# Hybrid encoder with experts on one core: one operand of convolutions, series and norms in PSUM, idle products on TensorE, GpSimd's splits behind the norm's root

## Chip, cores and metric

The kernel runs on one core of a Trainium2 chip. The metric is the time of one execution on the device in microseconds; a lower number is better. The engines are called PE (TensorE), DVE (VectorE), ACT (ScalarE), POOL (GpSimd) and SP (SyncE, which issues most DMAs).

## What is computed

The reference is a stack of two layers on 256 tokens of width 1024, all in float32. A layer mixes tokens in three branches, merges them with gates, and applies 32 SwiGLU experts, of which each token uses two.

```python
h = _layernorm(x, ln0_g, ln0_b)
for l in range(DEPTH):                       # DEPTH = 2
    mix = _mixer(h, w_in[l], ...)            # projections, three branches, gates, w_out
    h = _layernorm(DN_ALPHA * h + mix, ln1_g[l], ln1_b[l])
    ffn = _moe(h, w_router, router_bias, w1[l], w3[l], w2[l])
    h = _layernorm(DN_ALPHA * h + ffn, ln2_g[l], ln2_b[l])
...
# branch A: grouped-query attention; q and k get an RMS norm per head and an axial rotary turn
q = _axial_rope(_rms(q, q_g), tables) * (HEAD_DIM ** -0.5)
k = _axial_rope(_rms(k, k_g), tables)
# branch C: gated delta rule; q, k, v first pass a short convolution and SiLU
qkv = jax.nn.silu(_short_conv(jnp.concatenate([q, k, v], axis=-1), conv_w))   # 5 taps
g = -jnp.exp(A_log) * jax.nn.softplus(aa + dt_bias)                           # decay
# experts
hid = jax.nn.silu(xt @ w1[e]) * (xt @ w3[e])
y = y + comb[:, e:e + 1] * (hid @ w2[e])
```

The mixer's projections go in the order ga0, cqk, cz, cv, akv, aq, ga1, bqk, ...: cqk and cv are q, k and v of branch C, akv and aq the keys, values and queries of branch A, ga a gate.

## The kernel before

**Layers and tiles.** Tokens lie on the partitions in two tiles of 128 (t = 0, 1). Each layer has a mixer (about 265 us) and an expert stage (about 440 us). Weights are streamed from HBM by SP into rings; the slots of the experts' slabs come free as earlier work is done with what lies there.

**Splits.** Matrix products are made from a high and a low part. `split` (L186) casts a block of weights to the high part (ACT, `uh_...`) and subtracts it from the block for the low part (`ul_...`), on DVE or POOL. Products with three such terms follow on PE. A projection's weights come in four blocks u, two k steps each. `cut()` makes the next split of the stream, `take()` hands out the block.

**Order.** PE's order is written out by the program (`pinned`). The order on DVE, ACT and POOL is made by a scheduler; each engine works through its own queue in order.

**The mixer's first part.** `norm(t)` normalises tile t: `bn` takes statistics, `rsqrt` (L229) makes the root on POOL, `centred` (L252) subtracts the mean and multiplies by the gain, `shifted` (L257) multiplies by the root and adds the bias. Then `turn_in` transposes the tile (tp; the high part placeT, the low part placeU) and ga0 runs on it. `conv(i, b)` (L537) works on a bank b of 128 x 512 (two channel groups of 256 tokens): ACT copies it from PSUM into `placeH` (L541), DVE makes five taps for each group (one `ts`, four `stt`, into placeA or placeB), ACT takes tanh, DVE multiplies (into placeB or placeC).

`delta_line` (L608) makes the decay g. The logarithm in softplus is a series of eleven DVE operations on 128 x 16 elements, in the buffer shown as `gap`. From g follow POOL's products placeG and placeC and PE's products eb and db. `norm_rope` (L555) is the RMS norm and rotary turn of a key or query; for the key it runs twice (t = 0, 1) and ends in placeG. `key_line` then transposes the keys (kTA) on PE. The names placeA to placeU are ring places that several tensors share in turn.

**The expert stage.** After the mixer's norm, the router's choice `both` is made on DVE, the products `rk` count ranks, `select` makes the permutation P, `gather` brings tokens to the experts (xg on PE, copied to h), and `weigh` makes the weighted W, whose transpose is PT. Then for every expert: `up` (PE products named h), `down` (PE products named mo into two column halves n = 0, 1, evicted as the high part op by ACT and the low part by DVE), and for every second `combine` (my). After the last expert come the statistics of `my` and the next layer's norm, or the final one.

```python
for hf in range(2):                                   # down(e)
    w2 = slab()
    for j in range(2):
        for n in range(2):
            mm(bs[n][n * 64:n * 64 + 64], hidT[e][:, j, hf * 64:hf * 64 + 64],
               w2[:, j, n * 512:(n + 1) * 512], hf == 0 and j == 0, hf == 1 and j == 1)
```

In layer 1 three splits of ga0's blocks are issued ahead of the first norm, which is ordered behind the first of them (on DVE); the two others are POOL's ul_ga.

## Time and profile before

| | |
|---|---|
| runs | 1452.72, 1455.88, 1452.26 us (median 1452.72) |
| the profiled execution | 1453.74 us, its span 1452.1 us |
| mean granted clock of TensorE | 0.977 |
| busy: PE, DVE, ACT, POOL | 1340.0, 626.2, 404.1, 263.9 us |
| DMA | 479.89 MB, 330 GB/s over the span |

The span is the time from the first to the last instruction. Busy times are shares of different stages: PE and the DMA engines carry the expert stages, the other three mostly the mixers.

### The profile page before, as it was taken

What the parts mean: (1) busy time and instruction counts of PE and PEld (TensorE: products, weight loads), DVE (VectorE), ACT (ScalarE), POOL (GpSimd) and SP (SyncE); (2) the same over time, 40 slices, a digit from 0 to 9 for tenths busy, and PEclk for the clock granted to TensorE, in tenths of its full rate; (3) what the DMA queues carried; (4) which work ended last, traced back from release to release, by engine and by line L of the source; (5) the groups of instructions that cost most, each with busy time, mean ns of one, the idle gap of its engine ahead of it and who ended that gap; (6) DMA issues with size and microseconds to landing.
All of it is one profiled execution on the core that took longest, in us unless ns stands there. A gap on an engine that the chain in (4) does not pass through costs nothing. (4 is left out here: it accounts for less than half of the span.)

```text
span 1452.1 us, 23761 instructions
## 1 busy us (share of the span) xinstructions
PE 1340.0 (92%) x9708; PEld 892.1 (61%) x9708; DVE 626.2 (43%) x1218; ACT 404.1 (28%) x771; POOL 263.9 (18%) x327
## 2 busy tenths in 40 slices
PE   6879999899997999999788899998999899999986
PEld 5768777555554655555386777875555555555532
DVE  6887667612221222222269875774222222222213
ACT  3445543211111111111234455432111111111111
POOL 4485304300000000000026752033000000000000
PEclk9999999999999999999999899999999999999998
DMA  7534678799999999999845456796999999999995
GB/s 235 166 128 146 217 245 343 269 401 419 419 419 417 420 419 420 418 419 419 356 141 161 135 167 238 251 363 251 420 419 419 417 418 420 418 419 418 419 419 211
DMA packets 114533, 479.89 MB, mean 330 GB/s; under 512 B 25168, under 2 KB 38000, under 8 KB 65520
## 3 DMA queue, kind: packets, MB, share of 16 engines
q1 hardware_dynamic: 112464, 471.85, 83.1%
q0 software_dynamic: 1376, 5.24, 1.0%
q8 instruction: 81, 1.33, 0.4%
q10 hardware_dynamic: 576, 1.18, 0.2%
q14 instruction: 36, 0.29, 0.1%
HBM read 476.40 MB, written 1.84 MB: 329 GB/s over the span
## 5 line engine op out<-in xcount | busy, mean ns | idle before, releaser
L177 PE MATMUL h<-w,h 128*64 128x256 f32 x2016 | 232.8, 387 | 23.8 <-PEq L1390 9.7
L177 PEld LDWEIGHTS h<-w,h 128*64 128x64 f32 x2016 | 146.2, 139 | 101.7 <-issue 16.4
L171 DVE SCALAR_TENSOR_TENSOR hid<-gate,h 128x256 f32<-128x256 f32 x64 | 26.9, 421 | 405.3 <-ACT gate L1481 405.3
L171 DVE SCALAR_TENSOR_TENSOR op<-mo,rt,op 64x512 fp32r<-64x512 f32 x128 | 96.0, 750 | 222.3 <-ACT op L1511 221.4
L1511 ACT ACTIVATE op<-mo,rt 64x512 fp32r<-64x512 f32 x128 | 87.4, 683 | 311.8 <-PE mo L177 272.3
L177 PE MATMUL mo<-w,hidT 128*64 128x512 f32 x720 | 164.7, 596 | 4.1 <-DMA w<-in_w_dram 2.7
L162 POOL TENSOR_TENSOR W<-P,rt 128x128 f32<-128x128 f32 x64 | 24.2, 398 | 781.7 <-PE PT L183 708.5
L1481 ACT ACTIVATE gate<-h 128x256 f32<-128x256 f32 x64 | 24.5, 384 | 406.3 <-PE h L177 406.3
L177 PEld LDWEIGHTS mo<-w,hidT 128*64 128x64 f32 x720 | 51.3, 137 | 89.7 <-issue 76.3
L177 PE MATMUL h<-w,xg 128*64 128x256 f32 x864 | 96.9, 381 | 2.4 <-ACT h L1455 2.4
L177 PE MATMUL h<-wl,h 128*64 128x256 f32 x768 | 86.3, 381 | 2.2 <-ACT h L1455 1.5
L177 PEld LDWEIGHTS h<-w,xg 128*64 128x64 f32 x864 | 61.0, 137 | 34.3 <-ACT h L1455 3.9
L177 PEld LDWEIGHTS h<-wl,h 128*64 128x64 f32 x768 | 53.9, 137 | 30.6 <-ACT h L1455 2.4
L177 PE MATMUL mo<-wl,hidT 128*64 128x512 f32 x304 | 69.9, 597 | 2.9 <-DMA wl<-in_w_dram 2.9
L177 PE MATMUL my<-op,PT 128*128 128x512 f32 x256 | 69.3, 410 | 2.1 <-ACT op L1511 1.4
L177 PEld LDWEIGHTS my<-op,PT 128*128 128x128 f32 x256 | 45.4, 188 | 25.2 <-issue 11.5
L177 PE MATMUL xg<-P,hh 128*128 128x256 f32 x256 | 56.6, 304 | 1.9 <-DVE P L162 1.9
L177 PEld LDWEIGHTS xg<-P,hh 128*128 128x128 f32 x256 | 40.9, 196 | 25.6 <-issue 25.5
L177 PE MATMUL xg<-P,hl 128*128 128x256 f32 x256 | 52.9, 289 | 0.0
L177 PE MATMUL h<-wl,xg 128*64 128x256 f32 x416 | 47.9, 382 | 3.5 <-DMA wl<-in_w_dram 1.8
L177 PEld LDWEIGHTS mo<-wl,hidT 128*64 128x64 f32 x304 | 20.7, 137 | 37.7 <-issue 32.1
L177 PE MATMUL wo<-uh_wo,ym 128*128 128x512 f32 x128 | 41.4, 395 | 0.0
(443 smaller groups left out, 2449.2 us busy)
## 6 DMA issues: line engine op xcount, KB each, us to landing
w<-in_w_dram SPq DMA_DIRECT2D x268, 1024.0 KB, 19.9
wl<-in_w_dram SPq DMA_DIRECT2D x112, 1024.0 KB, 19.9
w_gb<-in_w_in_dram SPq DMA_DIRECT2D x16, 512.0 KB, 3.6
w_gc<-in_w_in_dram SPq DMA_DIRECT2D x16, 512.0 KB, 4.5
w_wo<-in_w_out_dram SPq DMA_DIRECT2D x16, 512.0 KB, 5.0
w_ga<-in_w_in_dram SPq DMA_DIRECT2D x14, 512.0 KB, 4.6
w_cqk<-in_w_in_dram SPq DMA_DIRECT2D x8, 512.0 KB, 3.5
w_aq<-in_w_in_dram SPq DMA_DIRECT2D x8, 512.0 KB, 4.4
```

The lines of the kernel that those rows point to most:

```text
L162: return eng.tensor_tensor(out=o, in0=x, in1=y, op=op).ins
L171: return V.scalar_tensor_tensor(out=o, in0=x, scalar=s, in1=y, op0=op0, op1=op1)
L177: ins = T.matmul(o, l, r, start=start, stop=stop, skip_group_check=True).ins
L1481: A.activation(g, b[:, :256], AF.Tanh, scale=0.5)
L1511: A.activation(hi, src, AF.Copy, scale=w)
```

## The change

Seven things change.

1. **Convolution.** The banks of cqk and cv are taken from another tag of PSUM, ACT's copy goes, the taps and the products read the bank itself, and tanh writes back into it. The five taps still add up in placeA or placeB in SBUF.
2. **Series.** Three of its quantities (`rr`, `sq_`, `acc`) lie in a PSUM bank `sb`; one product is added, so that no instruction has two operands in PSUM or two in SBUF where one can be in PSUM.
3. **Key's norm.** `norm_rope` reads the key from PSUM for the square and for the first product, without ACT's copy; the query keeps its copy.
4. **Layer norms on PSUM.** Where the source is PSUM (layer 1's first norm and the final one), `centred` writes in place in PSUM and `shifted` reads it there.
5. **Splits.** Between the layers only one split stands ahead of the norm; the two others follow its root.
6. **Last expert.** Its down products go by n: first all of the one column half, then the other.
7. **Idle products.** `keep_warm` makes products that nobody reads: 16 ahead of the first transposes in layer 0 (on zeros that DVE writes), 14 around the last combine of layer 0, in each layer 3 ahead of rk and 2 behind it.

```diff
@@ helpers
+WARM = 16, 14, 3, 2
+    def keep_warm(n, name, src=None):
+        b = bank("s", f"warm{name}")
+        src = cst[:, :256] if src is None else src
+        for _ in range(n):
+            T.matmul(b[:, :256], src[:, :128], src, start=True, stop=True, skip_group_check=True)
@@ centred, shifted
-        hs = h[:, t, n * 512:(n + 1) * 512]
-        stt(hs, src[n] if src else hs, mv[:, 0:1], gg[:, n * 512:(n + 1) * 512], OP.subtract, OP.mult)
+        hs = src[n] if src else h[:, t, n * 512:(n + 1) * 512]
+        stt(hs, hs, mv[:, 0:1], gg[:, n * 512:(n + 1) * 512], OP.subtract, OP.mult)
-        scope["normalised"] = stt(hs, hs, mv[:, 2:3], gb[:, n * 512:(n + 1) * 512], OP.mult, OP.add).ins
+        scope["normalised"] = stt(hs, src[n] if src else hs, mv[:, 2:3], gb[:, n * 512:(n + 1) * 512], OP.mult, OP.add).ins
@@ mixer
-                early.enter_context(tc.issue_after([cut() for _ in range(3)][0][1]))
+                early.enter_context(tc.issue_after(cut()[1]))
+        if l == 0:
+            with tc.high_priority(offset=PRI):
+                V.memset(mix[:, 0, :256], 0.0)
+            keep_warm(WARM[0], f"m{l}", mix[:, 0, :256])
+        else:
+            keep_warm(WARM[1], f"m{l}")
         with tc.high_priority(offset=PRI):
             with early:
                 norm(0)
+            if l:
+                with tc.issue_after(scope["rsqrt"].ins):
+                    [cut() for _ in range(2)]
@@ conv
-            bv = of(f"ring{i % 2}", 2, S)
-            with tc.high_priority(offset=PRI):
-                A.copy(bv.rearrange("p m s -> p (m s)"), b)
+            bv = b.rearrange("p (m s) -> p m s", m=2)
@@ norm_rope
-            A.copy(x[:, :n * 64], b)
             xv = x8(x[:, :n * 64])
+            raw = x8(b) if which else xv
+            if not which:
+                A.copy(x[:, :n * 64], b)
-            A.activation(sq[:, :n * 64], x[:, :n * 64], AF.Square)
+            A.activation(sq[:, :n * 64], b if which else x[:, :n * 64], AF.Square)
-            tt(V, xv, xv, rs[:, :n, None].to_broadcast([128, n, 64]), OP.mult)
+            tt(V, xv, raw, rs[:, :n, None].to_broadcast([128, n, 64]), OP.mult)
@@ delta_line
-            xx, ax, ee, rr, ss, pp, acc, g = (sc[:, i] for i in range(8))
+            xx, ax, ee, ss, pp, g = (sc[:, i] for i in range(6))
+            sb = bank("s", f"sb{l}")
+            rr, sq_, acc = (sb[:, 16 * i:16 * i + 16] for i in range(3))
+            tt(V, sq_, ee, rr, OP.mult)
             tt(V, ss, ee, rr, OP.mult)
-            tt(V, pp, ss, ss, OP.mult)
+            tt(V, pp, sq_, ss, OP.mult)
@@ projections
-                    bs = [bank("acc", f"cqk{l}{i}") for i in range(2)]
+                    bs = [bank("s", f"cqk{l}{i}") for i in range(2)]
-                    vbank = bank("acc", f"cv{l}")
+                    vbank = bank("s", f"cv{l}")
@@ moe
+        keep_warm(WARM[2], f"c{l}")
         b = bank("s", f"rk{l}")
@@ down
+            w2s = [slab() for _ in range(2)]
+            steps = [(hf, j, n) for hf in range(2) for j in range(2) for n in range(2)]
+            if e == NE - 1:
+                steps.sort(key=lambda x: x[2])
+            for hf, j, n in steps:
+                mm(bs[n][n * 64:n * 64 + 64], hidT[e][:, j, hf * 64:hf * 64 + 64],
+                   w2s[hf][:, j, n * 512:(n + 1) * 512], hf == 0 and j == 0, hf == 1 and j == 1)
@@ moe, ahead of select
+            keep_warm(WARM[3], f"g{l}")
```

The scheduler's orders move with it. On DVE in layer 0, behind the taps of the third convolution (placeA), before: g is the line that reads placeK, and the first split ul_ga stands behind both of its products.

```order
L166 TENSOR_SCALAR gap_83<-gap_83 128x16
L166 TENSOR_SCALAR gap_83<-gap_83,placeK_109 128x16
L171 SCALAR_TENSOR_TENSOR placeC_100<-placeH_105,placeA_99 128x512
L162 TENSOR_TENSOR placeH_105<-placeH_105,placeA_99 128x128
L166 TENSOR_SCALAR gap_83<-gap_83,placeK_109 128x16
L187 TENSOR_TENSOR ul_ga_755<-w_ga_692,uh_ga_754 128x1024
L162 TENSOR_TENSOR placeG_106<-placeH_105 128x2x64
L564 TENSOR_REDUCE placeS_108<-placeH_105 128x2
```

The same place now. The series steps are those on `sb`, the third convolution's source is `cv`, and the key's reduce is L582.

```order
L173 SCALAR_TENSOR_TENSOR placeC_100<-cv_513,placeA_99 128x512
L173 SCALAR_TENSOR_TENSOR sb_606<-sb_606,gap_83 128x16
L164 TENSOR_TENSOR placeH_105<-placeH_105,placeA_99 128x128
L173 SCALAR_TENSOR_TENSOR sb_606<-sb_606,gap_83 128x16
L164 TENSOR_TENSOR placeG_106<-placeH_105 128x2x64
L173 SCALAR_TENSOR_TENSOR sb_606<-sb_606,gap_83 128x16
L189 TENSOR_TENSOR ul_ga_868<-w_ga_767,uh_ga_867 128x1024
L164 TENSOR_TENSOR gap_83<-sb_606,gap_83 128x16
L582 TENSOR_REDUCE placeS_108<-placeH_105 128x2
L168 TENSOR_SCALAR gap_83<-gap_83 128x16
L170 TENSOR_SCALAR placeS_108<-placeS_108 128x2
L168 TENSOR_SCALAR gap_83<-gap_83,placeK_109 128x16 x2
```

Three splits ul_ga (two of them ahead of this piece) now stand ahead of g, and the second half of the key's norm is begun ahead of it.

On POOL at the same place, before: the products with g (into placeG and placeC) run on end, and the root of the second key half (the row with mhalf) comes behind them.

```order
L162 TENSOR_TENSOR placeH_105<-placeH_105,placeA_99 128x4x16 x2
L162 TENSOR_TENSOR placeG_106<-gap_83,placeK_109 128x512 x2
L162 TENSOR_TENSOR placeC_100<-gap_83,placeK_109 128x512
L233 TENSOR_TENSOR placeS_108<-placeS_108,mhalf 128x2
L162 TENSOR_TENSOR placeH_105<-placeH_105,placeA_99 128x4x16 x2
```

Now:

```order
L164 TENSOR_TENSOR placeH_105<-placeH_105,placeA_99 128x4x16 x2
L164 TENSOR_TENSOR placeG_106<-gap_83,placeK_109 128x512
L242 TENSOR_TENSOR placeS_108<-placeS_108,mhalf 128x2
L164 TENSOR_TENSOR placeG_106<-gap_83,placeK_109 128x512
L164 TENSOR_TENSOR placeC_100<-gap_83,placeK_109 128x512
L164 TENSOR_TENSOR placeH_105<-placeH_105,placeA_99 128x4x16 x2
```

The root moved between the first and the second product with g.

On PE at the end of layer 0's experts, before: the down products of the last expert (mo, two banks in turn), and what follows.

```order
L177 MATMUL mo_5854<-w_5856,hidT_5852 64x512
L177 MATMUL mo_5855<-w_5856,hidT_5852 64x512
L177 MATMUL mo_5854<-w_5856,hidT_5852 64x512
L177 MATMUL mo_5855<-w_5856,hidT_5852 64x512
L177 MATMUL mo_5854<-w_5862,hidT_5852 64x512
L177 MATMUL mo_5855<-w_5862,hidT_5852 64x512
L177 MATMUL mo_5854<-w_5862,hidT_5852 64x512
L177 MATMUL mo_5855<-w_5862,hidT_5852 64x512
L177 MATMUL my_2734<-op_5844,PT_5828 128x512 x2
L177 MATMUL my_2735<-op_5844,PT_5828 128x512 x2
L177 MATMUL my_2736<-op_5844,PT_5828 128x512 x2
L177 MATMUL my_2737<-op_5844,PT_5828 128x512 x2
```

Now:

```order
L179 MATMUL mo_5876<-w_5878,hidT_5874 64x512 x2
L179 MATMUL mo_5876<-w_5880,hidT_5874 64x512 x2
L179 MATMUL mo_5877<-w_5878,hidT_5874 64x512 x2
L179 MATMUL mo_5877<-w_5880,hidT_5874 64x512 x2
L231 MATMUL warmm_5949<-cst 128x256 x2
L179 MATMUL my_2749<-op_5866,PT_5850 128x512
L231 MATMUL warmm_5949<-cst 128x256
L179 MATMUL my_2749<-op_5866,PT_5850 128x512
L179 MATMUL my_2750<-op_5866,PT_5850 128x512
L231 MATMUL warmm_5949<-cst 128x256
L179 MATMUL my_2750<-op_5866,PT_5850 128x512
```

The down products go bank by bank, and idle products stand among the products my; ten more follow the last my, ahead of the transposes tp.

On POOL between the layers, before: the splits of ga0 and the root of the first norm (the row with stats).

```order
L187 TENSOR_TENSOR ul_ga_5928<-w_ga_5919,uh_ga_5927 128x1024
L233 TENSOR_TENSOR stats_5886<-stats_5886,mhalf 128x1
L187 TENSOR_TENSOR ul_ga_5932<-w_ga_5921,uh_ga_5931 128x1024
L445 MEMSET placeS_5914 128x128 x4
L166 TENSOR_SCALAR placeS_5914<-placeS_5914 128x30
```

Now:

```order
L242 TENSOR_TENSOR stats_5908<-stats_5908,mhalf 128x1
L189 TENSOR_TENSOR ul_ga_5974<-w_ga_5941,uh_ga_5973 128x1024
L189 TENSOR_TENSOR ul_ga_5978<-w_ga_5943,uh_ga_5977 128x1024
L463 MEMSET placeS_5936 128x128 x4
L242 TENSOR_TENSOR stats_5909<-stats_5909,mhalf 128x1
```

The root stands ahead of both splits.

## Rows read from the trace of the kernel before

**Rows 1.** Stretches of 20 us, all engines; columns: window, length, each engine busy (instructions), clock, DMA.

```profile
60.00:80.00 20.00, 16.24 (x68) 11.97 (x66) 18.33 (x35) 7.12 (x13) 12.69 (x10) 0.91 0.50 164
...
260.00:280.00 20.00, 15.92 (x97) 10.54 (x97) 16.64 (x47) 8.81 (x16) 11.02 (x11) 0.84 0.71 279
...
300.00:320.00 20.00, 19.64 (x156) 11.73 (x154) 4.69 (x8) 4.29 (x9) 0.00 (x0) 1.00 1.01 420
```

**Rows 2.** Timeline of PE, 52 to 116 us: start, duration, instruction, [idle before <-releaser].

```profile
81.74 0.66 PE L183 MATMUL kTA<-cst,placeG 128*128 128x128 f32 x4 [2.33 <-ACT gap L669]
```

**Rows 3.** Groups by form, DVE, 740 to 800 us: count, busy us, mean ns, idle before.

```profile
L171 DVE SCALAR_TENSOR_TENSOR gap<-gap 128x16 f32<-128x16 f32 x11 | 6.2, 562 | 0.0
...
L171 DVE SCALAR_TENSOR_TENSOR placeB<-placeH,placeS,placeB 128x255 f32<-128x255 f32 x4 | 4.0, 990 | 0.0
L171 DVE SCALAR_TENSOR_TENSOR placeB<-placeH,placeS,placeB 128x254 f32<-128x254 f32 x4 | 3.9, 993 | 0.0
...
L171 DVE SCALAR_TENSOR_TENSOR placeA<-placeH,placeS,placeA 128x255 f32<-128x255 f32 x8 | 3.7, 476 | 0.0
L187 DVE TENSOR_TENSOR ul_ga<-w_ga,uh_ga 128x1024 fp32r<-128x1024 f32 x3 | 3.6, 1214 | 0.0
...
L166 DVE TENSOR_SCALAR placeA<-placeH,placeS 128x256 f32<-128x256 f32 x4 | 1.3, 344 | 1.5 <-ACT placeH L541 1.5
...
L171 DVE SCALAR_TENSOR_TENSOR placeG<-placeG,cz 128x256 f32<-128x256 f32 x2 | 0.8, 418 | 0.1
```

**Rows 4.** Timeline of DVE, 42 to 82 us.

```profile
60.30 2.35 DVE L171 SCALAR_TENSOR_TENSOR gap<-gap 128x16 f32<-128x16 f32 x1
...
64.58 0.16 DVE L171 SCALAR_TENSOR_TENSOR gap<-gap 128x16 f32<-128x16 f32 x1
...
72.07 0.38 DVE L166 TENSOR_SCALAR gap<-gap,placeK 128x16 f32<-128x16 f32 x1
```

**Rows 5.** Timeline of POOL, 42 to 82 us.

```profile
60.03 2.58 POOL L187 TENSOR_TENSOR ul_aq<-w_aq,uh_aq 128x1024 fp32r<-128x1024 f32 x1 [1.38 <-ACT uh_aq L187]
...
73.19 2.09 POOL L162 TENSOR_TENSOR placeG<-gap,placeK 128x512 f32<-128x512 f32 x2
...
77.96 0.70 POOL L233 TENSOR_TENSOR placeS<-placeS,mhalf 128x2 f32<-128x2 f32 x1 [0.62 <-DVE placeS L168]
79.13 1.45 POOL L162 TENSOR_TENSOR placeH<-placeH,placeA 128x64 f32<-128x64 f32 x2 [0.47 <-DVE placeH L162]
```

**Rows 6.** Groups by form, DVE, the whole run.

```profile
L166 DVE TENSOR_SCALAR PT<-PT 128x256 fp32r<-128x256 f32 x32 | 13.3, 414 | 0.0
```

**Rows 7.** Timeline of all engines, 0 to 24 us.

```profile
16.14 3.41 DVE L187 TENSOR_TENSOR ul_ga<-w_ga,uh_ga 128x1024 fp32r<-128x1024 f32 x1
```

**Rows 8.** Stretches of 1 us at the entry of the experts of layer 0.

```profile
274.00:275.00 1.00, 0.68 (x2) 0.67 (x3) 0.96 (x4) 0.21 (x1) 1.00 (x2) 0.50 1.03 434
```

**Rows 9.** Timeline of all engines, 264 to 285 us.

```profile
273.10 0.18 PE L177 MATMUL rk<-both,before 128*128 128x32 bf16 x1 [1.72 <-DVE both L171]
...
276.50 0.76 POOL L162 TENSOR_TENSOR W<-P,rt 128x128 f32<-128x128 f32 x2 [0.39 <-DVE fl L1554]
...
278.55 2.81 PE L177 MATMUL h<-wl0op,h 128*64 128x256 f32 x16
...
281.19 1.89 PE L177 MATMUL h<-w,h 128*64 128x256 f32 x16
```

**Rows 10.** Timeline of all engines, 714 to 742 us.

```profile
726.00 0.55 POOL L233 TENSOR_TENSOR stats<-stats,mhalf 128x1 f32<-128x1 f32 x1
...
726.58 3.48 DVE L171 SCALAR_TENSOR_TENSOR h<-h,stats,gains 128x512 f32<-128x512 f32 x2
...
729.55 1.94 PE L183 MATMUL tp<-cst,h 128*128 128x128 f32 x8 [6.04 <-DVE h L171]
```

**Rows 11.** Timeline of all engines, 1430 to 1453 us.

```profile
1433.72 3.72 PE L177 MATMUL mo<-w,hidT 128*64 128x512 f32 x16 [0.72 <-ACT hidT L1493]
...
1438.12 1.54 DVE L171 SCALAR_TENSOR_TENSOR op<-mo,rt,op 64x512 fp32r<-64x512 f32 x2 [2.42 <-ACT op L1511]
```

More of the change, by code (lines that the diff above doesn't have):

```diff
@@ L252, in centred, with shifted @@
     def centred(t, n, gg, mv, src=None):
+        hs = src[n] if src else h[:, t, n * 512:(n + 1) * 512]
+        stt(hs, hs, mv[:, 0:1], gg[:, n * 512:(n + 1) * 512], OP.subtract, OP.mult)
+    def shifted(t, n, gb, mv, src=None):
         hs = h[:, t, n * 512:(n + 1) * 512]
-        stt(hs, src[n] if src else hs, mv[:, 0:1], gg[:, n * 512:(n + 1) * 512], OP.subtract, OP.mult)
-    def shifted(t, n, gb, mv):
-        hs = h[:, t, n * 512:(n + 1) * 512]
-        scope["normalised"] = stt(hs, hs, mv[:, 2:3], gb[:, n * 512:(n + 1) * 512], OP.mult, OP.add).ins
+        scope["normalised"] = stt(hs, src[n] if src else hs, mv[:, 2:3], gb[:, n * 512:(n + 1) * 512], OP.mult, OP.add).ins
     def normalise(t, gg, gb, mv, src=None):
@@ L265, in normalise @@
         for n in range(2):
-            shifted(t, n, gb, mv)
+            shifted(t, n, gb, mv, src)
     def stream(srcs, first, beside):
@@ L1497, in down @@
             bs = [bs[0], bs[-1]]
-            for hf in range(2):
-                w2 = slab()
-                for j in range(2):
-                    for n in range(2):
-                        mm(bs[n][n * 64:n * 64 + 64], hidT[e][:, j, hf * 64:hf * 64 + 64],
-                           w2[:, j, n * 512:(n + 1) * 512], hf == 0 and j == 0, hf == 1 and j == 1)
+            w2s = [slab() for _ in range(2)]
[5 more added lines that the diff above has]
+                   w2s[hf][:, j, n * 512:(n + 1) * 512], hf == 0 and j == 0, hf == 1 and j == 1)
             p = e // 2
```

## The prediction

> **What bounds the kernel now.** I read the table of stretches first. For most of the run TensorE is full or the DMA engines are: in an expert stretch the queues move 420 GB/s at full share [rows 1], so an expert layer ends a fixed time after its first slabs come free, and the first experts free them. A microsecond won in a mixer or in the entry of an expert layer is therefore a microsecond at the end. In the mixer's first 140 us TensorE is not full: in 60 to 80 us it is busy 16.24 of 20 while VectorE is busy 18.33 [rows 1]. The timeline of TensorE names the last such wait of that stretch: the transposes kTA of the normalised keys start at 81.74 after 2.33 us of idle [rows 2]. What they wait for comes from VectorE's queue: the logarithm series of delta_line, the third convolution, and behind them the rotary products of the key.
>
> So the change is worth what it takes out of VectorE's queue there, and I asked which instructions of it are longer than they need be. The groups by form, here those of layer 1, show the same operation at two prices: the eight taps into placeB take 0.99 us each, the sixteen into placeA 0.475; the eleven series steps on 16 columns have a mean of 0.56 [rows 3], though one alone takes 0.16 and another of the same form 2.35 [rows 4]. The long one starts 0.27 us after a GpSimd split (ul_aq, 2.58 us) and ends with it [rows 4, 5]. An operation with both tensor operands in SBUF and a GpSimd instruction shut each other out.
>
> **Mixer, both layers.** The conv taps and the series steps now have one operand in PSUM. What that returns: 8 x (0.99 - 0.475) = 4.1 us for placeB and 11 x (0.56 - 0.16) = 4.4 us for the series [rows 3, 4], 8.5 us of VectorE per layer.
>
> [...]
>
> What the operand itself costs has a row on either side: a scalar_tensor_tensor that reads PSUM takes 0.418 us for 256 columns where the tap takes 0.475 for 255, so 0.06 less [rows 3]; a tensor_scalar takes 0.414 from PSUM [rows 6] and 0.344 from SBUF [rows 3], so 0.07 more. Of some 50 operations that change per layer 24 are taps of the first kind, which gives -1.4 us; the other 26 at +0.07 give +1.8. I take zero and keep -3 to +3.5 (all fifty at one price).
>
> [...]
>
> Against the 8.5 us: VectorE's new order puts three splits ul_ga ahead of the gate factor g (before, they stood behind it), 3 x 1.21 = 3.6 us [rows 3]; one extra product (0.2) and the rest of the first key half (three small operations, 0.3 each, 0.9). The splits have two SBUF operands and stand where GpSimd runs its two ul_aq: a split that meets one took 3.41 us instead of 1.21 [rows 7], 2.2 more. One or two can meet; I take one. And VectorE will wait more for ScalarE's casts, whose weights arrive no sooner than slots come free; 1.0 us is my choice (0 to 3). g before was ready at 72.07 + 0.38 = 72.45 [rows 4]; now at 72.45 - 8.5 + 3.6 + 0.2 + 0.9 + 2.2 + 1.0 = 71.85.
>
> From g to kTA took 9.3 us [rows 2, 4], with VectorE's second key half in the middle. In the new order that half's root stands between GpSimd's first and second product with g, so GpSimd does 1.05 + 0.70 + 2 x 1.05 + 1.45 = 5.3 us without a gap, and from its last product to kTA it is 81.74 - 80.58 = 1.16 as before [rows 2, 5]: 6.5, against 9.3. kTA then starts at 78.3, **3.4 us sooner**. Later waits in this mixer hang on the same VectorE queue, so I carry the shift to the end. Two layers: -6.8. The ScalarE copies that vanish (three of conv, two of the key per layer) shorten the way from a projection to its taps and count inside the wait above. Waits of aq on its splits go as well, and buy nothing while kTA is behind VectorE.
>
> **Entry of the experts.** [...] **-1.7 per layer**, -3.4. The bounds are 0 (clock falls anyway) and -2.4 (W sooner too).
>
> **Last expert, sorted.** Before, the sixteen product records of the last down ran in pairs on the two column halves: 3.72 us, 0.23 each [rows 11]. I read that as two at a time, 0.43 to 0.46 each alone. Sorted, n = 0 ends where both ended, and n = 1 takes its 8 x 0.43 = 3.4 after that: 7.16 us. Its copy on ScalarE (1438.12 - 1437.44 = 0.68) and the low part on VectorE (0.77) follow, 8.6 us after the start; before, both were through 1438.12 + 1.54 - 1433.72 = 5.94 after it [rows 11]. VectorE's queue has the n = 1 low part ahead of the statistics, so those start **2.7 us later**. At the kernel's end nothing hides that: +2.7. Below: if a pair does not share the array, sorting costs nothing and n = 0 is evicted earlier, -0.7.
>
> **Between the layers.** The same +2.7. GpSimd's root no longer stands behind a split (it started at 726.00 with no idle ahead [rows 10]): -0.6. The shifted pass took 3.48 us for two halves, locked out by the other split; the first half takes 0.7 with PSUM as source: the transposes come 2.15 sooner after the root. With ten idle products ahead of them they run at the higher clock: the eight took 1.94 [rows 10], about 1.0 then, -0.9. VectorE's own ul_ga now meets the split that was pushed behind the root: +0.7. Sum **-0.3**; bounds -3 (split hidden) and +2.7 (nothing given back).
>
> **Start.** The sixteen idle products make the first transposes faster, for nothing: the first gate tile waits for VectorE's ul_ga, through at 16.14 + 3.41 = 19.55 [rows 7], whatever the clock. 0.
>
> **Sum:** -6.8 - 3.4 + 2.7 - 0.3 = -7.8 us. The profiled execution took 1453.74 us (span 1452.1), 1.0 above the median of 1452.72; from the median: **1444.9 us**. No change that can be told is within 0.3%, 4.4 us.
>
> **Rivals.**
> *A, the forecast:* 1439 to 1449, chance 0.44.
> *B, the mixer gives nothing:* the fifty operations at the dearer price, or VectorE short of casts, eat the 3.4 per layer. For it speaks the 0.07 of the tensor_scalar; against it that 24 of the fifty are taps. Then -3.4 + 2.7 - 0.3 = -1.0: 1451.7. Chance 0.26; 0.05 of that with the clock falling as well (1455).
> *C, slower:* the three splits stand in the middle of the series, and the lock moves to them: VectorE's share of the 8.5 that is truly returned is f. The mixer gives -8.5 f + 5.1 per layer (all other terms as above). At f = 0.6 it is zero, below 0.3 the whole is slower by over 4.4 us; at f = 0.15 it is 2 x 3.8 - 1.0 = +6.6: 1459.3. For it speaks that GpSimd's splits remain where they are; against it that most placeB and series steps can no longer meet them. Chance 0.12.
> *D, larger:* no split meets another and VectorE never waits: 3.2 more per layer, -14.2: 1438.5, and 1435 if sorting is free. TensorE's rows in 140 us and later would have to follow. Chance 0.18.
>
> **Range:** 1434 to 1456, from D to where B ends; about 0.12 is left above and 0.06 below. A's own is 1439 to 1449. Faster: A but for its edge, and D, 0.60; same: B and A's edge, 0.28; slower: C, 0.12.
>
> **What the new profile would show.** Taps into placeB near 0.42 and no series step above 0.3; if they are 0.5 and more, B. Three ul_ga of VectorE at 1.2 to 3.4 before 75 us; if the sum of their excess is over 4 us, C. kTA near 78.3 with a shorter wait in both layers. Granted clock 1.0 through 273 to 280 us, and the first sixteen h products in 1.9 us. mo of expert 31 in about 7.2 us, not 3.7. The shifted pass between the layers at 1.4 us, and tp(0) at 1.0. The sum is wrong if the shift of kTA is not found again in the transposes qTA at 105 us or at the mixer's end, or if the first slab of the experts is asked for no sooner.

## The result, and the profile after

The changed kernel takes 1436.62 us (median of 4 runs, 1434.16 to 1437.54), the kernel before 1453.5 beside it: a ratio of 0.9879, interval 0.9861 to 0.9898. That is 17 us less, where 7.8 were forecast. The profiled execution has a span of 1435.9 us, 16.2 less than before.

The stretches that answer to [rows 1], same columns:

```profile
60.00:80.00 20.00, 16.58 (x71) 11.63 (x70) 18.45 (x52) 9.35 (x19) 10.88 (x13) 0.91 0.59 183
...
260.00:280.00 20.00, 18.24 (x119) 12.02 (x121) 12.18 (x39) 6.73 (x11) 10.21 (x10) 1.00 0.63 240
```

VectorE is as busy as before in 60 to 80 us, but gets through 52 instructions instead of 35. The groups by form on VectorE, 730 to 790 us, against [rows 3]:

```profile
L189 DVE TENSOR_TENSOR ul_ga<-w_ga,uh_ga 128x1024 fp32r<-128x1024 f32 x4 | 4.8, 1212 | 0.0
...
L173 DVE SCALAR_TENSOR_TENSOR placeB<-cqk,placeS,placeB 128x254 f32<-128x254 f32 x4 | 1.9, 476 | 0.0
...
L173 DVE SCALAR_TENSOR_TENSOR sb<-sb,gap 128x16 f32<-128x16 f32 x10 | 1.7, 172 | 0.0
...
L170 DVE TENSOR_SCALAR placeS<-placeS 128x16 f32<-128x16 f32 x1 | 1.3, 1269 | 0.0
...
L168 DVE TENSOR_SCALAR placeB<-cqk,placeS 128x256 f32<-128x256 f32 x2 | 0.9, 475 | 0.0
```

A tap into placeB takes 0.476 us instead of 0.99, a series step 0.172 instead of 0.562, and no split ul_ga meets another. The row of 1.27 us on 16 columns shows that the lock is not gone: it is a tensor_scalar from SBUF to SBUF (763.29 to 764.56), beside GpSimd's product placeG (762.26 to 764.53), and took 0.39 and 0.40 in the kernel before.

The timeline of VectorE in layer 0, from the three splits that were moved ahead of g to the first decay mask (placeB<-placeB,placeK):

```profile
64.77 1.22 DVE L189 TENSOR_TENSOR ul_ga<-w_ga,uh_ga 128x1024 fp32r<-128x1024 f32 x1
...
66.74 1.22 DVE L189 TENSOR_TENSOR ul_ga<-w_ga,uh_ga 128x1024 fp32r<-128x1024 f32 x1
...
69.24 1.22 DVE L189 TENSOR_TENSOR ul_ga<-w_ga,uh_ga 128x1024 fp32r<-128x1024 f32 x1
...
70.65 0.17 DVE L168 TENSOR_SCALAR gap<-gap 128x16 f32<-128x16 f32 x1
...
77.88 0.69 DVE L164 TENSOR_TENSOR placeB<-placeB,placeK 128x512 f32<-128x512 f32 x1 [0.86 <-ACT placeB L709]
```

The line at 70.65 is g, after its change of sign. The line that reads placeK, which the section on the change calls g, is only the first product made from it. And the transposes of TensorE that [rows 2] showed at 81.74:

```profile
76.84 0.27 PE L185 MATMUL kTA<-cst,placeG 128*128 128x128 f32 x1
77.40 0.55 PE L185 MATMUL kTA<-cst,placeG 128*128 128x128 f32 x3 [0.28 <-ACT placeG L604]
```

They come 4.9 us sooner; the masks come 6.7 sooner. What stood in front of the masks before is not among the rows on record, so here is that piece of the kernel before, VectorE again (the line at 71.87 is g):

```profile
71.87 0.17 DVE L166 TENSOR_SCALAR gap<-gap 128x16 f32<-128x16 f32 x1
...
80.94 0.29 DVE L162 TENSOR_TENSOR placeG<-placeH 128x128 f32<-128x128 f32 x1
81.15 1.22 DVE L187 TENSOR_TENSOR ul_ga<-w_ga,uh_ga 128x1024 fp32r<-128x1024 f32 x1
82.28 1.26 DVE L171 SCALAR_TENSOR_TENSOR placeS<-gap,placeS 64x4 f32<-64x4 f32 x1
...
84.54 0.16 DVE L162 TENSOR_TENSOR placeS<-gap,placeS 128x8 f32<-128x8 f32 x1
84.62 0.68 DVE L162 TENSOR_TENSOR placeB<-placeB,placeK 128x512 f32<-128x512 f32 x1
```

From 80.94 on no row has a wait: before, the masks came when VectorE's queue had run down to them. Now they wait 0.86 us for ScalarE, which works on TensorE's products made from g.

The prediction named the query transposes qTA as the place where the shift must be found again. Before and now (TensorE):

```profile
108.54 0.90 PE L183 MATMUL qTA<-cst,placeE 128*128 128x128 f32 x3 [3.53 <-DVE placeE L162]
...
101.82 0.90 PE L185 MATMUL qTA<-cst,placeE 128*128 128x128 f32 x3 [3.53 <-DVE placeE L164]
```

They come 6.7 us sooner, like the masks, behind the same wait for VectorE.

The entry of the experts in layer 0 ([rows 8, 9]; warmc and warmg are the idle products):

```profile
264.75 1.46 PE L231 MATMUL warmc<-cst 128*128 128x256 f32 x6
...
266.64 0.18 PE L179 MATMUL rk<-both,before 128*128 128x32 bf16 x1 [0.43 <-DVE both L173]
...
266.77 1.11 PE L231 MATMUL warmg<-cst 128*128 128x256 f32 x4
...
271.30 1.95 PE L179 MATMUL h<-wl0op,h 128*64 128x256 f32 x16
```

The wait ahead of rk is 0.43 us, the granted clock stays at 1.00, and the first sixteen h products take 1.95 us, not 2.81. Between the layers ([rows 10]), all engines:

```profile
717.28 4.48 PE L231 MATMUL warmm<-cst 128*128 128x256 f32 x20
...
719.04 5.68 POOL L189 TENSOR_TENSOR ul_ga<-w_ga,uh_ga 128x1024 fp32r<-128x1024 f32 x2
719.68 1.40 DVE L173 SCALAR_TENSOR_TENSOR h<-my,stats,gains 128x512 f32<-128x512 f32 x2
721.00 1.48 DVE L189 TENSOR_TENSOR ul_ga<-w_ga,uh_ga 128x1024 fp32r<-128x1024 f32 x1
721.60 1.04 PE L185 MATMUL tp<-cst,h 128*128 128x128 f32 x8
```

The shifted pass takes 1.40 for two halves and the transposes 1.04. The lock fell on GpSimd's splits (5.68 for two that took 2.35 and 2.33 before), not on VectorE's (1.48, where the four of 730 to 790 us took 1.21 each). The last expert of layer 1 ([rows 11]), with the two column halves one after the other:

```profile
1416.55 5.42 PE L179 MATMUL mo<-w,hidT 128*64 128x512 f32 x16 [0.72 <-ACT hidT L1516]
...
1420.23 0.68 ACT L1535 ACTIVATE op<-mo,rt 64x512 fp32r<-64x512 f32 x1 [2.50 <-PE mo L179]
...
1422.72 0.76 DVE L173 SCALAR_TENSOR_TENSOR op<-mo,rt,op 64x512 fp32r<-64x512 f32 x1 [1.03 <-ACT op L1535]
```

The second low part is through 6.93 us after the start of mo, where it was 5.94.

Where the 16.2 us lie is read from start times in the two timelines: the first rk of each layer, the second run of sixteen h, the transposes of layer 1's second token tile (tp1), the first of the products my that run beside the last expert. The same for the runs told below (us, from each profiled execution; experts: from the sixteen h to the next mark):

| kernel | mixer 0 to rk | entry 0 | experts 0, to tp1 | tp1 to rk 1 | entry 1 | experts 1 | end | span |
|---|---|---|---|---|---|---|---|---|
| before | 273.10 | 8.09 | 457.08 | 251.35 | 8.23 | 428.85 | 25.40 | 1452.1 |
| after | 266.64 | 6.44 | 455.64 | 244.68 | 6.39 | 429.73 | 26.38 | 1435.9 |
| e5, the change again | 266.95 | 6.44 | 454.11 | 245.64 | 6.38 | 428.18 | 26.70 | 1434.4 |
| e1 | 272.98 | 6.36 | 455.30 | 251.60 | 6.36 | 429.30 | 26.30 | 1448.2 |
| e8 | 271.03 | 8.15 | 456.56 | 248.77 | 8.11 | 429.35 | 25.43 | 1447.4 |
| e9 | 266.04 | 6.65 | 456.13 | 242.41 | 7.06 | 429.38 | 25.33 | 1433.0 |
| e10 | 267.18 | 6.34 | 457.02 | 242.84 | 6.38 | 429.72 | 26.32 | 1435.8 |
| e11 | 265.64 | 6.36 | 455.69 | 241.93 | 6.36 | 429.53 | 26.29 | 1431.8 |
| e12 | 269.55 | 6.44 | 454.00 | 248.43 | 6.37 | 428.14 | 26.87 | 1439.8 |
| e16 | 266.36 | 6.36 | 454.73 | 244.81 | 6.35 | 429.15 | 26.34 | 1434.1 |

The two mixers give 6.46 and 6.67 us (forecast 3.4 each), the entries 1.65 and 1.84 (1.7), experts and the part between the layers 1.44 and -0.88, the end -1.0 (-2.7). The rows of the change and of e5, the same program, show how far such a part wanders: 1 to 1.5 us. Nor is a profiled execution the median: that of the change is the longest of its four, those of e9 and e12 are the shortest of theirs.

### The profile page after: what moved, and what is told of

Same layout as the page of the kernel before. It is cut to its first block, busy times and chain, and to the rows that moved or that the text cites. A ratio compares the mean times of both kernels' runs of the same rounds, so it can differ in the third digit from the quotient of the medians.

```text
span 1435.9 us, 23914 instructions
## 1 busy us (share of the span) xinstructions
PE 1349.3 (94%) x9788; PEld 894.9 (62%) x9788; DVE 613.6 (43%) x1221; ACT 399.2 (28%) x761; POOL 256.5 (18%) x327
## 3 DMA queue, kind: packets, MB, share of 16 engines
HBM read 476.40 MB, written 1.84 MB: 333 GB/s over the span
## 5 line engine op out<-in xcount | busy, mean ns | idle before, releaser
L179 PE MATMUL mo<-w,hidT 128*64 128x512 f32 x720 | 167.8, 595 | 3.6 <-DMA w<-in_w_dram 1.6
L179 PEld LDWEIGHTS h<-wl,xg 128*64 128x64 f32 x416 | 28.6, 137 | 22.7 <-DMA wl<-in_w_dram 6.8
```

The costliest lines, as they stand in the source:

```text
L179: ins = T.matmul(o, l, r, start=start, stop=stop, skip_group_check=True).ins
```

## The experiments

Theories: **Q**, everything that stands in VectorE's queue up to the decay masks bounds a mixer, so lock time returned there counts in full, and moving work within that queue costs nothing. **R**, the forecast's account: a mixer gives 3.4, and other parts give the rest. P and O (e4) say that the place of the splits decides, in the one direction or the other.

**The three mixer edits undone (e1).** In the changed kernel (this cut and the next ones are abridged):

```diff
-            bv = b.rearrange("p (m s) -> p m s", m=2)
+            bv = of(f"ring{i % 2}", 2, S)          # with ACT's copy again
-            rr, sq_, acc = (sb[:, 16 * i:16 * i + 16] for i in range(3))
+            rr, sq_, acc = sc[:, 6], sc[:, 7], sc[:, 1]
-            raw = x8(b) if which else xv
+            raw = xv                               # with ACT's copy for the key too
```

> The changed kernel with the three mixer edits undone: convolution, series and key norm take all operands from SBUF again, with ScalarE's copies; sort, idle products, layer norms in PSUM and the order of the splits stay. Theory Q (VectorE's whole queue up to the decay masks bounds the first part of the mixer, and what counts is its total length, locks included): the locks of 8.5 us per layer come back, less the 2 that the changed kernel still has, so 12 to 14 us over the changed kernel, 1449 to 1451. Rival R (the mixer gave the 3.4 us per layer that were forecast, and the rest came from elsewhere): 7 us, about 1443.5.

1450.27 us, ratio 0.998 (0.9969 to 0.9991): by the ratios 14.7 of 17.6 us are gone. Groups by form on VectorE, 742 to 802 us:

```profile
L173 DVE SCALAR_TENSOR_TENSOR gap<-gap 128x16 f32<-128x16 f32 x11 | 6.2, 564 | 0.1
L173 DVE SCALAR_TENSOR_TENSOR placeB<-placeH,placeS,placeB 128x255 f32<-128x255 f32 x4 | 4.0, 988 | 0.0
```

The locked prices are back and both mixers last as before (table). Q's size holds, R falls. The idle products at the entry are still in it: with the mixers of before they give 1.73 and 1.87 us.

**One of them undone: the series (e2), the convolutions (e3).** The same lines, one edit at a time.

> Only the series back in SBUF. Theory Q: two or three steps per layer meet a GpSimd split again at about 2.2 us each, and all of it lies on the queue that bounds: 6 to 9 us over the changed kernel. Rival (the steps are short and stand where VectorE waits anyway): under 2 us.

> Only the convolution back in SBUF, with ScalarE's copy. Theory Q: the placeB taps meet GpSimd's ul_cv again, 4.1 us per layer, and GpSimd's three ul_cv take 7 us instead of 4: 6 to 9 us over the changed kernel; with e2 it should add up to e1 within 2 us. Rival (taps ahead of the convolution's last product are hidden behind the wait for the akv and aq splits): under 3 us.

e2: 1440.25, ratio 0.992 (0.9902 to 0.9938); e3: 1447.34, ratio 0.9964 (0.9952 to 0.9977). By the ratios 6.0 and 12.3 us, together more than the 14.7 of both, so the parts don't add, and e3 is above the 6 to 9 that were expected. In e2's trace the eleven steps took 0.177 (735 to 795 us) although their operands are in SBUF, but other operations of the series took 1.48 and 2.38 (58.74 and 61.75 us): what one edit leaves locked seems to depend on where the other puts the instructions.

**g ahead of the splits (e4).** The low parts of the three ul_ga are ordered behind g:

```diff
+                with tc.issue_after(scope["g"]) if i in (24, 25, 26) else ExitStack():
+                    lo = eng.tensor_tensor(out=u[1], in0=w, in1=u[0].bitcast(F32), op=OP.subtract).ins
```

> The changed kernel with VectorE's three ul_ga held back until the series has made g; nothing else changes, so VectorE's total work up to the decay masks stays. Theory Q: within 1.5 us of the changed kernel, though g and GpSimd's products come up to 3.6 us sooner. Rival P (the forecast's own path: the moment of g decides through GpSimd's products and the key): up to 7 us faster. Rival O (the new order of the splits was the gain): up to 7 us slower.

1438.04, ratio 0.990 (0.9883 to 0.9917), span 1433.9: not told apart from the change. g was ready 2.5 us sooner and GpSimd's first product with it came 0.9 sooner, but kTA 2.9 later, the masks 1.6 later, rk 0.75 later. TensorE (eb) and VectorE (masks):

```profile
73.58 0.61 PE L179 MATMUL eb<-gap,placeK 128*128 128x16 f32 x2 [4.12 <-DVE gap L168]
...
79.46 0.69 DVE L164 TENSOR_TENSOR placeB<-placeB,placeK 128x512 f32<-128x512 f32 x1 [2.59 <-ACT placeB L712]
```

The splits now stand ahead of VectorE's two products of g with placeK, and eb waits for these: what is taken from in front of g stands behind it. P and O fall. Q is right in the size, but at the masks VectorE waits 2.59 us for ScalarE. What comes last there is no longer the end of its queue, as in the kernel before, but what TensorE and ScalarE make from g; in the change it is so by 0.86.

**The change again (e5), the last expert unsorted (e6), no idle products at the entry (e7).**

```diff
-            if e == NE - 1:                        # e6
-                steps.sort(key=lambda x: x[2])
-WARM = 16, 14, 3, 2
+WARM = 16, 14, 0, 0                                # e7
```

> The changed kernel itself, on the same chip as the next three, so that they can be compared with it: about 1436 us, ratio 0.988.

> The changed kernel with the last expert's down products in pairs again. In its trace the sorted products and their eviction took 6.93 us and 5.94 before the change, so theory S (sorting costs 1.0 us at the kernel's end, and as much between the layers where the transposes follow the statistics): 1 to 2 us faster than the changed kernel. Rival (between the layers the sorted order pays, because idle products and first evictions fill the gap): no change or up to 1 us slower.

> The changed kernel without the idle products ahead of rk and behind it, in both layers. Theory: the clock falls to 0.50 as before, h starts 0.8 us later and its first sixteen products take 2.8 instead of 1.95 us, 1.7 us per layer: 3 to 4 us slower than the changed kernel. Rival (the clock stays up because less idle time is left ahead of rk anyway, 0.43 instead of 1.72 us): within 1 us.

e5: 1434.27, ratio 0.9865 (0.9846 to 0.9884). e6: 1434.48, 0.9873 (0.9856 to 0.989); its end takes 25.34 us, 1.0 less than with the sort, the size that the profile of the change showed, but its time is not told apart from e5's. e7: 1438.35, 0.9903 (0.9884 to 0.9922), 4 us over e5; its trace shows only 0.3 to 0.4 in each entry (6.72 and 6.79 against 6.44 and 6.38), so the times and the trace don't agree on the size.

**The kernel before with GpSimd's splits of cv and aq on VectorE (e8), the change with the same (e12).**

```diff
-POOL = (1, 2, 5, 13, 14, 15, 17, 18, 21, 23, 50, 62)
+POOL = (1, 2, 5, 17, 18, 50, 62)
```

> The kernel before, operands as they were, with GpSimd's five splits of cv and aq moved to VectorE. VectorE gets 3 x 0.6 + 2 x 1.14 = 4.1 us more work per layer. Theory L (what made its taps and series long are those five splits of GpSimd): the 8.5 us per layer go, net up to -4.4 per layer, 3 to 9 us faster than before. Rival M (an operand in SBUF is dear by itself): 4.1 more per layer, about 8 us slower than before.

> The changed kernel with GpSimd's splits of cv and aq (five per layer) done on VectorE, as was done with the kernel before. Five more splits are 3 x 0.65 + 2 x 1.21 = 4.4 us or more of VectorE's queue per layer. Theory L (what the change leaves of the lock up to the masks is about 6.4 us per layer, part of it by these splits): 3 to 4.5 us come back, so 0 to 1.5 per layer dearer, 0 to +3 in all. Rival M (the change has taken out nearly all lock that these splits made): the full 4.4 per layer, +8 to +9. Rival N (PE waits for ScalarE's casts and not for VectorE there): no difference within 1 us.

e8: 1448.45, ratio 0.9967 (0.9955 to 0.9979), faster though VectorE got five splits more. Groups by form, 740 to 800 us:

```profile
L171 DVE SCALAR_TENSOR_TENSOR gap<-gap 128x16 f32<-128x16 f32 x11 | 1.9, 168 | 0.1
```

e12: 1442.36, ratio 0.9934 (0.9918 to 0.9951), slower than the change by 5.7 us in the medians and 8.0 by the ratios. VectorE's timeline has the splits at

```profile
44.60 0.69 DVE L189 TENSOR_TENSOR ul_cv<-w_cv,uh_cv 128x512 fp32r<-128x512 f32 x1
...
55.31 1.23 DVE L189 TENSOR_TENSOR ul_aq<-w_aq,uh_aq 128x1024 fp32r<-128x1024 f32 x1 [0.32 <-ACT uh_aq L189]
```

so the five are 3 x 0.69 + 2 x 1.23 = 4.5 us. In the kernel before a mixer got 2.1 and 2.6 us shorter by them (table): they made 6.6 to 7.1 us of lock. In the change it gets 2.9 and 3.7 longer: they make 0.8 to 1.6. The difference, 5 to 6.3 us per mixer, is nearly what the mixers gained, from a pair of runs that shares nothing with e1; by the ratios it is 6.4. L holds for e8; e12 lies between L and M, nearer M.

**The mixer edits alone (e9), and the change without the part between the layers (e10).** e9 is the kernel before with convolutions, series and key changed, nothing else. e10 is the change with `centred` and `shifted` in SBUF, three splits ahead of the norm and `WARM = 16, 0, 3, 2`.

> The kernel before with the three mixer edits alone (convolutions, series and key's norm read PSUM); no idle products, norms, splits and last expert as before. Theory Q (VectorE's whole queue up to the decay masks bounds the mixer, so the lock time returned there counts in full): each mixer about 6.5 us shorter, -12 to -13.5 us against before, 1440 us or a little less; the first h about 7 us sooner than before's 278.55 less nothing for the entry, so near 272, with the granted clock still at 0.50 there. Rival W (the mixer edits give only the forecast's 3.4 per layer, the rest came from idle products and order): -7 us, 1446.

> The changed kernel with the parts between the layers undone: norms in SBUF, three splits ahead of the norm, no 14 idle products (the sorted last expert and the rest stay). Theory: the boundary gives 1.5 to 2.5 us in all, so from the start of mo of expert 31 to the first transposes of the second tile goes from 20.5 back to 22 or 23 us, and the time is 1.5 to 2.5 above the change; in the trace the shifted pass takes 3.5 us for two halves and the transposes about 1.9 us for eight. Rival (the forecast's boundary of -0.3): within 0.5 us of the change.

e9: 1438.65, ratio 0.9912 (0.9896 to 0.9929), -13.4 us; its profiled execution, the shortest of its four, has 1433.0. Q's size, W falls. Its entries surprise: 6.65 and 7.06 without any idle product. The clock there (stretches of 1 us, as [rows 8]):

```profile
268.00:269.00 1.00, 1.00 (x6) 1.00 (x6) 1.00 (x1) 0.02 (x1) 1.00 (x1) 0.50 0.22 82
...
270.00:271.00 1.00, 1.00 (x10) 0.83 (x10) 0.20 (x1) 0.37 (x1) 0.19 (x1) 0.91 0.00 0
271.00:272.00 1.00, 1.00 (x10) 0.68 (x12) 0.88 (x3) 0.37 (x1) 0.76 (x2) 1.00 0.00 0
```

It fell after the same wait of 1.72 us and was back 4 us behind rk. e10: 1438.27, ratio 0.9908 (0.9891 to 0.9925), span 1435.8. Its tp1 comes 1.4 to 2.9 us later after the experts, as expected, but its second mixer is 1.8 to 2.8 shorter than the change's. By the spans the part between the layers gives nothing. By the times it gives something: e10's median is 1.6 above the change's, its ratio 0.003 above the change's and 0.004 above e5's (4 and 6 us; its interval overlaps the change's and is clear of e5's).

**Less of the series under the lock (e11).**

```diff
-            A.activation(beta, ba[:, 0]..., AF.Tanh, scale=0.5)
-            ts(V, beta, beta, 0.5, OP.mult, 0.5, OP.add)
+            A.activation(braw, ba[:, 0]..., AF.Tanh, scale=0.5)    # braw in the PSUM bank sb
+            ts(V, beta, braw, 0.5, OP.mult, 0.5, OP.add)
+                A.mul(ea, ea, -1.0)                                # g's sign, on ACT
-            ts(V, g, g, -1.0, OP.mult)
-            V.tensor_copy(kds[:, 0], edl[:, 0])
+            A.copy(kds[:, 0], edl[:, 0])
```

> The changed kernel, with three more small operations of the decay line taken out of the lock: ACT's tanh for beta writes into the PSUM bank of the series and VectorE reads it there, the minus sign of g is put into the factor by ACT, and the copy of the decays is ACT's. Theory K (what stands in VectorE's queue ahead of g is on the path): the beta step falls from 1.17 to about 0.2 us and one step goes, g 1 us sooner, 0.5 to 1.3 us per mixer, -1 to -2.6 in all, a ratio of 0.986 or less. Rival S (casts or PE bound it there, or GpSimd's lock moves to the next small operation): within 1 us of the change.

1433.43, ratio 0.9871 (0.9855 to 0.9888): not told apart from the change. VectorE, 48 to 60 us:

```profile
52.49 1.17 DVE L168 TENSOR_SCALAR gap<-gap 128x16 f32<-128x16 f32 x1
...
56.96 0.16 DVE L170 TENSOR_SCALAR placeS<-sb 128x16 f32<-128x16 f32 x1
...
59.48 2.18 DVE L189 TENSOR_TENSOR ul_aq<-w_aq,uh_aq 128x1024 fp32r<-128x1024 f32 x1 [0.93 <-ACT uh_aq L189]
```

Beta's step fell from 1.26 to 0.16, but the next split then waits 0.93 us for ScalarE's cast and takes 2.18 anyway (2.00 in the change, beside GpSimd's ul_aq), and GpSimd's first product with g starts at 70.89, as in the change (70.90). The earlier g of K did not come; S fits. The span of 1431.8 owes most to a shorter second mixer (table), of which more below.

**Idle products in the wait for the query (e13 to e18).** In the change TensorE waits 3.53 us for the second query transposes and then shows a clock of 0.50 up to gr (101 to 106 us). `keep_warm(24)` stood behind the first transpose in e13 (the change), e14 (e11) and e15 (e9 with the entry's idle products), `keep_warm(6)` in e16, e17 and e18.

> The changed kernel with 24 idle products behind the first query transpose, in TensorE's wait for the second (3.53 us in layer 0, 3.52 in layer 1). Theory V (the clock falls in that wait and takes about 2 us back): granted clock 1.00 through 98 to 106 us, the twelve bqk products behind the wait 0.28 and not 0.41 each, gr 1.5 to 2.3 us sooner in each layer, -3 to -4.5 in all, about 1431. Rival U (behind gr something else waits, such as the softmax on ScalarE or the weights, or the idle products end later than the wait): gr earlier or not, rk within 0.7 of the change, time within 1.5 us of it.

> The same idle products in the kernel e11_series_less_locked. In e11 the clock fell in layer 0 alone (0.50 in 102 to 104 us) and not in layer 1. Theory V: 1 to 2 us less than e11 (span 1431.8), from layer 0 alone, about 1430 to 1432 by the median. Rival U: the same as e11 within 1 us.

> The kernel before with the mixer edits, the five idle products at the experts' entry and the 24 at the query; norms, splits between the layers and the last expert as before. Theory V2 (the edits between the layers are worth their 1.7 to 2.5 us only when no later wait of the mixer takes them back): against e9 (span 1433.0) the entry gives 0.3 to 0.7 per layer and nothing is given at the query, whose clock already stayed at 1.00, so span 1431 to 1432.5; then e13 should be below it by about the boundary's 2 us. Rival: e13 and this one within 1 us, so the edits between the layers give nothing at all.

1448.35, 1447.55 and 1448.76 us: 10 to 14 above the change, e11 and e9, because the idle products were far too long. TensorE in e13:

```profile
98.22 10.59 PE L231 MATMUL warmq<-cst 128*128 128x256 f32 x48
```

One idle product on 256 columns is two records of 0.22 us, 0.44 in all. With 6:

> The changed kernel with 6 idle products (12 records of 0.22 us, 2.65 us) in TensorE's wait for the second query transposes. Theory V: they end at about 101 us, 0.8 ahead of the wait's end at 101.8, the granted clock stays at 1.00 to gr, which comes 1.5 us sooner in each layer: -2 to -3 in all, about 1432. Rival U (what follows gr waits for another engine): rk within 0.7 us of the change, the same time within 1.5.

> The same 6 in the kernel e11_series_less_locked (span 1431.8), whose clock fell behind that wait in layer 0 alone, for some 3 us. Theory V: 0.5 to 1.5 less than e11, about 1431 to 1432.5 by the median. Rival U: the same within 1.

> The kernel before with the mixer edits, the five idle products at the experts' entry and 6 at the query; norms, splits between the layers and last expert as before. The 6 should do nothing here (the clock stayed at 1.00 in e9). If the edits between the layers are worth 2 us when no fall of the clock takes them back, e16 is about 2 below this one less 1.0 for its sorted last expert, so 1 us; if they are worth nothing, e16 is 1 above it. Either within about 1434 to 1437 by the median (e9 1438.65 less 0.3 to 0.7 per layer at the entry, its span 1433.0).

1435.96 (0.988, 0.9864 to 0.9897), 1434.10 (0.9862, 0.9845 to 0.9878) and 1436.22 (0.9883, 0.9867 to 0.99). TensorE in e16:

```profile
98.47 2.75 PE L231 MATMUL warmq<-cst 128*128 128x256 f32 x12
101.42 0.55 PE L185 MATMUL qTA<-cst,placeE 128*128 128x128 f32 x3 [0.19 <-DVE placeE L164]
...
103.33 1.10 PE L179 MATMUL gr<-placeD 64*64 64x128 f32 x32
```

The clock stayed at 1.00, and gr came at 103.33 and 809.22 instead of 105.21 and 812.33: V's first step. But rk came only 0.3 and 1.1 us sooner, and the time is the change's, as U has it. U's reason is not what the traces show, though: TensorE keeps the 1.9 us of layer 0 for 124 us, up to the transposes tpm of the merged branches. These in the change, then in e16, with a stretch of e16 behind them:

```profile
230.51 0.98 PE L185 MATMUL tpm<-cst,mix 128*128 128x128 f32 x7 [0.73 <-POOL mix L164]
...
228.63 1.52 PE L185 MATMUL tpm<-cst,mix 128*128 128x128 f32 x7 [0.73 <-POOL mix L164]
...
230.00:231.00 1.00, 1.00 (x4) 0.81 (x4) 0.84 (x2) 0.60 (x1) 1.00 (x1) 0.50 0.99 416
```

Behind the same short waits the granted clock stayed at 1.00 in the change and was 0.50 from 229 to 232 us in e16. From the first tpm to the first product with w_out it took 4.84 us instead of 3.25, so 1.6 of the 1.9 were lost there; in layer 1 it took 4.30 instead of 3.24. In e9, e17 and e18 the clock fell at that place in one layer each, in e10 and e11 in none; what decides it, no run shows. So the mixer's end does hang on gr, and what was won there was taken back by a later fall of the clock. e16 is 0.3 us below e18 by the medians, midway between the two expectations for what the edits between the layers are worth; with two falls of the clock in e16 and one in e18 it decides nothing. No version here is faster than the change by more than the runs can tell.

## Why the prediction was wrong

**What bounds.** Right in the main: VectorE's queue and the lock, shown by e1, e8 and e12, and the shift is found again at the query transposes (6.7) and at the mixer's end (6.5).

**Mixer.** Here the forecast failed. Of the 8.5 us of lock 6.5 arrived at the mixers' ends, not 3.4. The step that failed is "Against the 8.5 us: ... 3 x 1.21 = 3.6 us", with the key's half (0.9) beside it: both were charged as a loss because they moved ahead of g. They had stood behind g before, in the same queue, ahead of the masks; one of the three is the row at 81.15 above. From g to the masks it was 84.62 - (71.87 + 0.17) = 12.6 us before and is 77.88 - (70.65 + 0.17) = 7.1 now. (The 72.45 that the prediction takes for g is the end of the first product made from it.) "I carry the shift to the end" then took the shift at kTA (4.9 when measured) for the whole, and it was 6.7 at the masks. e4 shows from the other side that the place of the splits is not worth their 3.6 us. Why 6.5 arrived and not 8.5 is seen in the two timelines of layer 0: other operations ahead of the masks ran beside GpSimd, and what they took above the price of the same form alone grew from about 4.3 to 6.5 us (an estimate from the durations; now beta's step with 1.26, the second ul_aq with 2.00 and a copy of 8 columns with 1.14 are among them). Smaller terms: no ul_ga met a split (2.2 charged; three at 1.22), but that ul_aq did, for 0.8; of the 1.0 for ScalarE's casts one wait of 0.43 is seen ahead of g; g came 1.2 us sooner (70.82 for 72.04), not 0.6. The operand itself: a tap from PSUM costs what it cost from SBUF (0.476 against 0.476 [rows 3]), a tensor_scalar on 256 columns 0.475 against 0.344, 0.13 more for six per layer, so 0.8 us where zero was taken.

The lock is also wider than the prediction has it, which speaks of two tensor operands in SBUF: a tensor_scalar with one took 1.17 us on 16 columns in e11 and in the change, there from 51.90 to 53.07, beside GpSimd's two ul_akv (50.30 to 53.03). The same form took 0.16 at 777.80, with no GpSimd instruction beside it.

**Entry.** Right in size: no run shows the 1.7 itself, and in its place the runs showed 1.65 and 1.84. In layer 0 the granted clock was 0.50 from 274 to 280 us before and stays at 1.00 now, the first sixteen h start 4.66 us behind rk instead of 5.45 and take 1.95 instead of 2.81. Right in cause, too, where the mixers are those of before (e1). With the new mixers the idle products are worth less: e9 has most of the gain without them, since the clock came back by itself 4 us behind rk there, and 7 before.

**Last expert.** Mis-sized: 1.0 us for 2.7. The first half ended where both had ended (ScalarE's copy of it starts 3.68 us after mo), but the second took 1.7 us more and not 3.4; mo took 5.42, not 7.16, and e6's trace confirms the 1.0.

**Between the layers.** From mo of the last expert to tp1 it is 20.50 us instead of 22.18, -1.7 for -0.3: the lock that was charged to VectorE's split (0.7) and to the late start (2.7) was 0.3 there and 1.0. The idle products end at 717.28 + 4.48 = 721.76, right where tp starts although h was through at 721.08: fourteen are about one too many. Whether this reaches the end is open. The times say so (e10), the profiled executions don't: the second mixers of e10 and e9, without these edits, are 1.8 to 3.2 us shorter. That difference lies at the query. Counted from tp1, the second query transposes start at 80.2 us in the change and at 79.0 in e10 and e9, and gr at 83.6 against 81.3 and 80.9, in the change with a granted clock of 0.50 (807 to 813 us), which stayed at 1.00 in e9; from gr to rk the four agree within 0.5 us, e11 being the fourth. e11 has the edits and its transposes start at 78.6, so the edits need not be the reason; it may be the scheduler's order there.

**Rivals.** D came nearest: 3.2 more per mixer, 1438.5. One condition held in part (no ul_ga met a split, one ul_aq did), but the gain did not come by a g that is still sooner, as D has it: most of it lay behind g. B and C fell with the taps and steps at 0.476 and 0.172; of the lock that C moves to the splits, the 0.8 of that ul_aq is seen.

## What to carry to other kernels

When work is moved within one engine's queue, price the queue up to the last consumer that waits for it, not only up to the one result that it was moved ahead of: what is added in front of g leaves the place behind g. To size a lock between two engines, move the other engine's work over once before and once after: the sum of both shifts is the lock that was removed (e8 and e12: 5 to 6.3 us per mixer). And when time won at one place does not reach the end, follow the shift from mark to mark until it is lost before naming the reason: at the query the first explanation (nothing hangs on it) was wrong, since the shift lasted to tpm and the clock took it there (1.6 of 1.9 us in layer 0 of e16).

## What I had not expected of the hardware

- The same local pattern (1.72 us of idle, then rk) gave some 6.8 us at the clock's lower level in the kernel before and 3.4 in e9 (summed over the rows of 1 us), and behind the same waits at tpm the clock was 0.50 in e16 and 1.00 in the change. What decides it is not shown by these runs.
- Two column halves done one after the other took 5.42 us, between the 3.72 measured for products in turn and the 7.16 that the prediction had estimated.
- A copy of 8 columns and six tensor_scalar of 2 or 16 columns, all in SBUF, took 1.14 to 1.35 us in the change's mixers, each beside a GpSimd instruction; alone a tensor_scalar of 16 columns took 0.16 or 0.17.
